# Output weights split by VectorE and spread over the attention's tail and the merge, with the first columns of two token tiles first

## The chip, the cores and the metric

The kernel runs on one NeuronCore of a Trainium2 chip. The metric is device microseconds of one execution; lower is better. Rows of the profile name the engines PE (TensorE matmul), PEld (TensorE weight load), DVE (VectorE), ACT (ScalarE), POOL (GpSimd) and SP (SyncE, which here only issues DMAs); a q behind a name (SPq, ACTq) is the engine's issuing queue.

## The reference, cut to what matters

```python
merged = sigmoid(g_conv) * y_conv + sigmoid(g_att) * y_att      # y_att = (att * silu(z_att)) @ w_att_out
x = x + gate * (merged @ w_o[layer])                            # 1024 tokens x 1024 columns, depth 1
return _rmsnorm(x, final_g)                                     # over each token's 1024 columns
```

Ahead of this stand a norm, one wide input projection, a convolution branch and an attention branch with 3 dilation groups of 8 heads. Everything is float32.

## The kernel before, in words

**Split operands.** A float32 product is made of three matmuls on fp32r tiles. Each operand is split into a high part (`hi`, a rounding copy on ACT, L57) and a low part (`lo = raw - hi`, a subtraction, L58, on DVE or, where `lo_eng` says so, on POOL); PE then adds hi*hi, hi*lo and lo*hi into one PSUM tile. Every weight block takes this road: SP loads it into a `wraw` buffer (three of them, used in turn), ACT writes `whi`, DVE or POOL writes `wlo`, and only then is the `wraw` buffer free for the next load.

**The last three stages.**

1. *The attention's tail.* PE's order is written by hand in slots; the other engines' order is made by a scheduler. After the last scores PE runs the gate projections (L73 to L75, tiles `whi`, `wlo`), with POOL making `wlo`. Beside them DVE combines the last head pair's three groups, in two halves of 512 tokens: `rd` is loaded (L885), reduced to `pr` (L897 to L922), four PE transposes of `pr` (L926) follow at a fixed place in PE's order, and from them come the last parts of `ah` and `al` (the attended rows' high and low parts).
2. *The merge* (`for d in range(KT)`). Per block `d` of 128 output features: 24 matmuls (two halves of 512 tokens, 12 each) of `w_ao[d]` with `ah`, `al`; per half DVE multiplies with the gate (L1034, `sgr`), adds the convolution's part (L1035, `ttr`), ACT writes `hh` and DVE `hl` (the merged rows' parts). DVE also makes the next block's `wlo`. `sgr` and `ttr` are loaded two blocks ahead, into four buffers of the tag `tmp`.
3. *The output* (`for t in range(8)`). For each tile `t` of 128 tokens, two halves `n` of 512 columns, each of 24 matmuls (L1059 to L1061): `hh`, `hl` of all 8 blocks k against the parts `oh`, `ol` of `w_o[n, kp]` with kp = k // 2. Then DVE and ACT apply gate, residual and norm (L1062 to L1074), and SP stores.

**The output weights before.** `w_out(n, kp)` loads one block of 128 x 1024, splits it with the low part on POOL, and is called for n = 0 at d = 1, 3, 5, 7 of the merge (tiles of their own) and for n = 1, four times, behind the merge (in the tiles of `ah` and `al`, tags s0 to s3, which the merge reads up to its end).

Of the kernel before, what the change touches and what calls it, by code (L numbers as in the profile page):

```python
# [8 lines left out]
F32 = mybir.dt.float32  # L9
F32R = mybir.dt.float32r  # L10
I32 = mybir.dt.int32
AF = mybir.ActivationFunctionType
# [4 lines left out]
P = 128  # L17
S = 1024
D = 1024
KT = 8  # L20
# [19 lines left out]
def layer(ctx: ExitStack, tc: tile.TileContext, a, out):  # L40
    nc = tc.nc
# [10 lines left out]
    def sbuf_pool(name, **kw):  # L52
        return tc.tile_pool(name=name, bufs=1, reuse_waits="tile", **kw)

    def split(hi, lo, raw, lo_eng=None):

        nc.scalar.activation(hi, raw, AF.Copy)  # L57
        (lo_eng or nc.vector).tensor_sub(lo, raw, hi.bitcast(F32))  # L58

    def load_raw(src, n=1024):  # L60
        raw = wpool.tile([P, n], F32, name="wraw", tag="wraw", bufs=3)
        nc.sync.dma_start(raw, src)
        return raw
# [16 lines left out]
    hh = const.tile([P, KT, S], F32R, name="hh")  # L80
    hl = const.tile([P, KT, S], F32R, name="hl")
# [37 lines left out]
    def bank():  # L119
        return pd.tile([P, 512], F32, name="d", tag="d")  # L120
# [50 lines left out]
    with sbuf_pool("start") as st, tc.manual_schedule(  # L171
# [125 lines left out]
        for raw in u_raw[0:2]:  # L297
            hi = wpool.tile([P, 1024], F32R, name="whi", tag="whi")
            lo = wpool.tile([P, 1024], F32R, name="wlo", tag="wlo")
# [35 lines left out]
        hi = st.tile([P, 1024], F32R, name="u2h", tag="tot")  # L335
        lo = st.tile([P, 1024], F32R, name="u2l", tag="vs", bufs=1)
# [3 lines left out]
        for kt in range(KT):  # L340
# [9 lines left out]
            c = slice(kt * P, (kt + 1) * P)  # L350
            for i, (wh, wl) in enumerate(u_w):
                for half in range(2):
                    s = slice(half * 512, half * 512 + 512)
# [121 lines left out]
    class Glu:  # L475
# [19 lines left out]
        def units(self):  # L495
            return [Unit(KT + self.ct, self.sig), Unit(self.ct, self.glu, HALF)]
# [127 lines left out]
    for d in range(KT):  # L624
        w, sg_ = ahead
# [19 lines left out]
    stk = ctx.enter_context(sbuf_pool("stacked"))  # L645
    ap_ = c_ctx.enter_context(sbuf_pool("att"))

    def pair_tile(n, name, dt=F32R):
        return stk.tile([P, 2, S], dt, name=name, tag=f"s{n}")
# [108 lines left out]
    def pieces():  # L758

        source = units()  # L760
        ahead = next(source)
        while ahead:
            (hi, lo), consume = ahead
            ahead = next(source, None)
            for half in range(2):
                s = slice(half * 512, half * 512 + 512)
                ps = bank()
                for k in range(KT):
                    c = slice(k * P, (k + 1) * P)
                    mm3(ps, hi[:, c], lo[:, c], hh[:, k, s], hl[:, k, s], k == 0, k == KT - 1)  # L770
                    if k == 3:
                        yield
                yield lambda half=half, s=s, ps=ps: consume(half, s, ps)
# [162 lines left out]
    def att_parts(j, s, raw):  # L936

        if j // 2 not in ah:
            ah[j // 2], al[j // 2] = pair_tile(j // 2, "ah"), pair_tile(2 + j // 2, "al")
        split(ah[j // 2][:, j % 2, s], al[j // 2][:, j % 2, s], raw)  # L940

    stream = pieces()


# [6 lines left out]
    with tc.manual_schedule(engines={nc.tensor.engine}):  # L951
        for slot_ in range(-LEAD, (2 * len(order) + KT) * 4 - LEAD):
            due, made[:] = made[:], []
            after = next(stream)
            for x in due:
                move_kq(*x)
                if x == (0, 1):
                    load_low(0)
            if 0 <= slot_ < stages:
                n, st_ = divmod(slot_, 8)  # L960
                if st_ == 0:
                    heads[n] = Attend(n)
                if st_ == 4 and n + 1 < len(order):
                    load_low(n + 1)
                heads[n].scores(st_)
            if TURN <= slot_ < stages + TURN:
                n, st_ = divmod(slot_ - TURN, 8)
                heads[n].turn(st_)
            if VAL <= slot_ < stages + VAL:
                n, st_ = divmod(slot_ - VAL, 8)  # L970
                heads[n].values(st_)
                if st_ == 7:
                    del heads[n]
                    j, g = order[n]
                    if g == 2:
                        for half, steps in enumerate((FIRST, SECOND)):
                            c = combine(j, half)
                            for x in steps:
                                beside.setdefault(slot_ + x, []).append(c)
            for c in beside.pop(slot_, ()):  # L980
                next(c)
            for c in late:
                for x in (2, 2, 3):
                    beside.setdefault(slot_ + x, []).append(c)
            late[:] = []
            j = slot_ - stages - VAL
            if 0 <= j < 3:
                raw = load_raw(atscr[j])
                for half in range(2):
                    s = slice(half * 512, half * 512 + 512)  # L990
                    att_parts(j, s, raw[:, s])
            if j == 11:
                ahead = weights(a["w_ao"][0], 512)
            if after:
                after()
        assert not beside and next(stream, None) is None
# [2 lines left out]

    pd = ctx.enter_context(psum_pool("pd3", bufs=8))  # L1000
    fp = ctx.enter_context(sbuf_pool("fin"))
    woh, wol, w1 = {}, {}, [None, None]

    def w_out(n, kp):
        raw = load_raw(a["w_o"][n, kp])
        if n:
            if kp % 2 == 0:
                w1[0:2] = pair_tile(kp // 2, "oh1"), pair_tile(2 + kp // 2, "ol1")
            hi, lo = (t[:, kp % 2] for t in w1)
        else:  # L1010
            hi, lo = (fp.tile([P, 1024], F32R, name=f"{x}{kp}") for x in ("oh", "ol"))
        split(hi, lo, raw, nc.gpsimd)
        woh[n, kp], wol[n, kp] = hi, lo

    def temp4(name):
        return fp.tile([P, S], F32, name=name, tag="tmp", bufs=4)

# [7 lines left out]
    for d in range(KT):  # L1025
        w, (sg_, tt) = ahead
        if d + 1 < KT:
            ahead = weights(a["w_ao"][d + 1], 512), gates_load(d + 1)
        if d % 2:
            w_out(0, d // 2)  # L1030
        hi, lo = hh[:, d, :], hl[:, d, :]

        def merge(half, s, ps):
            nc.vector.tensor_mul(sg_[:, s], ps, sg_[:, s])  # L1034
            nc.vector.tensor_add(tt[:, s], tt[:, s], sg_[:, s])  # L1035
            split(hi[:, s], lo[:, s], tt[:, s])

        project(w, merge, 4, lambda k, s: ah[k // 2][:, k % 2, s], lambda k, s: al[k // 2][:, k % 2, s])


    for kp in range(4):
        w_out(1, kp)
    gate_b = fp.tile([P, D], F32, name="gate_b")
    nc.sync.dma_start(gate_b, gscr.to_broadcast([P, D]))
    fg_b = fp.tile([P, D], F32, name="fg_b")
    nc.sync.dma_start(fg_b, a["final_g"].to_broadcast([P, D]))
    for t in range(8):
        xt, y = temp4("xt"), temp4("y")
        nc.sync.dma_start(xt, a["x"][t * P:(t + 1) * P, :])
        ss = fp.tile([P, 3], F32, name="ss", tag="ss", bufs=2)  # L1050
        cuts = (0, 512, 1024) if t < 7 else (0, 512, 768, 1024)
        for n, (c0, c1) in enumerate(zip(cuts, cuts[1:])):
            s = slice(c0, c1)
            ps = bank()[:, 0:c1 - c0]
            for k in range(KT):
                c = slice(t * P, (t + 1) * P)
                o = (k % 2) * 512 + c0 % 512
                rh, rl = (w[c0 // 512, k // 2][:, o:o + c1 - c0] for w in (woh, wol))
                nc.tensor.matmul(ps, hh[:, k, c], rh, start=k == 0, stop=False)  # L1059
                nc.tensor.matmul(ps, hh[:, k, c], rl, start=False, stop=False)  # L1060
                nc.tensor.matmul(ps, hl[:, k, c], rh, start=False, stop=k == KT - 1)  # L1061
            nc.vector.tensor_mul(y[:, s], ps, gate_b[:, s])  # L1062
            nc.vector.tensor_add(y[:, s], y[:, s], xt[:, s])
            nc.scalar.activation(xt[:, s], y[:, s], AF.Square, accum_out=ss[:, n:n + 1])
        r = fp.tile([P, 1], F32, name="r", tag="r", bufs=2)
        tmp = fp.tile([P, 3], F32, name="tmp3", tag="tmp3", bufs=2)
        nc.vector.tensor_add(r, ss[:, 0:1], ss[:, 1:2])
        if t == 7:
            nc.vector.tensor_add(r, r, ss[:, 2:3])
        nc.vector.tensor_scalar(r, r, 1.0 / D, EPS, op0=mult, op1=add)  # L1070
        inv_sqrt(r, 1, tmp)
        for n in range(2):
            s = slice(n * 512, n * 512 + 512)
            nc.vector.scalar_tensor_tensor(y[:, s], y[:, s], r, fg_b[:, s], op0=mult, op1=mult)  # L1074
            nc.sync.dma_start(out[t * P:(t + 1) * P, s], y[:, s])


# [64 lines left out]
```

## Time and profile before

| what | value |
|---|---|
| median of 3 timed runs | 1287.0 us (1286.51 to 1288.05) |
| the profiled execution's own time | 1284.9 us |
| its span, first to last instruction | 1283.1 us |
| PE busy in the span | 1251.0 us (97%) |
| DVE, ACT, POOL busy | 895.0, 476.3, 114.6 us |
| granted TensorE clock, mean | 0.999 of full speed |

Matmuls are pipelined: one of 512 columns is shown with 0.39 us, but the next starts 0.23 us behind it where nothing is missing. So the time that PE loses is read from the distance of starts. "Idle before" is the time in which an engine waited, with what ended it.

### The profile page before, as it was taken

The numbers are of one execution on the slowest core, as the hardware profiler recorded it, in microseconds if no ns is written. First come the engines' busy times: TensorE is split into PE (matmuls) and PEld (weight loads), VectorE is DVE, ScalarE is ACT, GpSimd is POOL, SyncE is SP. The second block draws the span as 40 slices with busy tenths as digits, with TensorE's granted clock in tenths as the row PEclk, the third lists the DMA queues.
The fourth block names the chain that finished last, engine by engine and source line by source line (L and its number), as shares of the span: only waits on it lengthen the run. The fifth ranks groups of instructions, "written<-read, shape, count | busy, mean of one in ns | idle before, by whom it ended". The sixth has DMA issues, their size and how long they took to land.

```text
span 1283.1 us, 16610 instructions
## 1 busy us (share of the span) xinstructions
PE 1251.0 (97%) x6148; PEld 1050.6 (82%) x6148; DVE 895.0 (70%) x1568; ACT 476.3 (37%) x911; POOL 114.6 (9%) x86
## 2 busy tenths in 40 slices
PE   6999999999999999999999999999999989999997
PEld 4777888888888888888788888888888878887786
DVE  6777999999999986853245545766666654348544
ACT  4653112111222146620115545445545458333211
POOL 0000000000000000000132111111111002202200
PEclk9999999999999999999999999999999999999999
DMA  9522311211211122555675565576675565558322
GB/s 367 180 97 73 109 66 57 91 52 47 94 55 50 50 74 74 165 183 188 143 182 125 125 159 142 156 179 150 153 207 126 147 181 177 151 203 286 117 96 69
DMA packets 85525, 171.53 MB, mean 134 GB/s; under 512 B 11202, under 2 KB 41026, under 8 KB 85444
## 3 DMA queue, kind: packets, MB, share of 16 engines
q1 hardware_dynamic: 69024, 157.66, 42.1%
q10 hardware_dynamic: 16420, 12.80, 3.2%
q8 instruction: 49, 0.80, 0.3%
q14 instruction: 32, 0.26, 0.1%
HBM read 105.74 MB, written 33.23 MB: 108 GB/s over the span
## 4 chain that ended last, share of the span: by engine, by line
PE 86%; DVE 5%; DMA 3%; issue 2%; ACT 2%; SPq 1%; POOL 1%; POOLq 0%; ACTq 0%; DVEq 0%
PE d L73 20%; PE d L74 20%; PE d L75 20%; PE o L875 4%; PE d L466 2%; PE d L467 2%; PE d L465 2%; PE d L1060 2%; PE d L1061 2%; PE t L860 2%; PE d L1059 2%; PE s L844 1%; PE s L843 1%; PE d L249 1%; PE d L247 1%
## 5 line engine op out<-in xcount | busy, mean ns | idle before, releaser
L73 PE MATMUL d<-hh,whi 128*128 128x512 f32 x1072 | 428.0, 399 | 1.8 <-DVE rot L710 0.9
L74 PE MATMUL d<-hl,whi 128*128 128x512 f32 x1072 | 418.0, 390 | 1.8 <-DVE hl L347 1.8
L75 PE MATMUL d<-hh,wlo 128*128 128x512 f32 x1072 | 419.1, 391 | 0.0
L406 DVE SCALAR_TENSOR_TENSOR v<-u,cw,v 128x1024 f32<-128x1024 f32 x232 | 280.7, 1287 | 0.0
L75 PEld LDWEIGHTS d<-hh,wlo 128*128 128x128 f32 x1072 | 201.3, 188 | 43.7 <-POOL wlo L58 0.7
L74 PEld LDWEIGHTS d<-hl,whi 128*128 128x128 f32 x1072 | 201.9, 188 | 41.6 <-DVE hl L347 2.6
L73 PEld LDWEIGHTS d<-hh,whi 128*128 128x128 f32 x1072 | 201.8, 188 | 41.3 <-DVE rot L710 1.5
L57 ACT ACTIVATE whi<-wraw 128x512 fp32r<-128x512 f32 (+1 forms) x107 | 87.9, 834 | 272.6 <-PE d L74 236.0
L58 POOL TENSOR_TENSOR wlo<-wraw,whi 128x512 fp32r<-128x512 f32 (+1 forms) x56 | 84.5, 1525 | 659.1 <-ACT whi L57 557.2
L852 ACT ACTIVATE sb<-sb,nm 128x128 f32<-128x128 f32 (+1 forms) x192 | 85.0, 444 | 86.3 <-DVE nm L850 82.0
L847 DVE CUSTOM_DVE_ANT_0 sb<-s,mask 128x128 f32<-128x128 f32 (+1 forms) x192 | 59.8, 347 | 61.1 <-PE s L844 54.9
L875 PE MATMUL o<-vt,pt 128*128 128x64 f32 x560 | 73.5, 267 | 1.6 <-ACT pt L863 1.0
L875 PEld LDWEIGHTS o<-vt,pt 128*128 128x128 f32 x560 | 70.2, 192 | 2.6 <-ACT pt L863 1.3
L58 DVE TENSOR_TENSOR wlo<-wraw,whi 128x1024 fp32r<-128x1024 f32 (+1 forms) x51 | 60.2, 1183 | 15.1 <-ACT whi L57 14.6
L1060 PE MATMUL d<-ol,hh 128*128 128x512 f32 (+1 forms) x136 | 51.6, 380 | 3.0 <-POOL ol L58 3.0
L844 PE MATMUL s<-k,ql 128*128 128x128 f32 (+1 forms) x192 | 51.0, 279 | 2.9 <-DMA ql<-kqp 2.9
L1059 PE MATMUL d<-oh,hh 128*128 128x512 f32 (+1 forms) x136 | 51.4, 378 | 0.1
L1061 PE MATMUL d<-oh,hl 128*128 128x512 f32 (+1 forms) x136 | 51.4, 378 | 0.0
L467 PE MATMUL d<-vh,hl 128*128 128x512 f32 x128 | 49.8, 389 | 0.0
L73 PE MATMUL d<-uh,whi 128*128 128x512 f32 x128 | 49.8, 389 | 0.0
L466 PE MATMUL d<-vl,hh 128*128 128x512 f32 x128 | 49.8, 389 | 0.0
L74 PE MATMUL d<-ul,whi 128*128 128x512 f32 x128 | 49.8, 389 | 0.0
(213 smaller groups left out, 1738.6 us busy)
## 6 DMA issues: line engine op xcount, KB each, us to landing
wraw<-in_w_t SPq DMA_DIRECT2D x67, 512.0 KB, 4.1
k<-kqp SPq DMA_DIRECT2D x96, 128.0 KB, 2.6
q<-kqp SPq DMA_DIRECT2D x96, 128.0 KB, 2.4
wa<-in_w_ada SPq DMA_DIRECT2D x16, 512.0 KB, 5.9
rd<-oscr SPq DMA_DIRECT2D x8, 792.0 KB, 5.6
ql<-kqp SPq DMA_DIRECT2D x48, 128.0 KB, 2.4
wraw<-in_w_v SPq DMA_DIRECT2D x11, 512.0 KB, 3.6
x<-in_xT SPq DMA_DIRECT2D x8, 512.0 KB, 10.2
```

The lines of the kernel that those rows point to most:

```text
L57: nc.scalar.activation(hi, raw, AF.Copy)
L58: (lo_eng or nc.vector).tensor_sub(lo, raw, hi.bitcast(F32))
L73: nc.tensor.matmul(ps, lh, rh, start=start, stop=False)
L74: nc.tensor.matmul(ps, lh, rl, start=False, stop=False)
L75: nc.tensor.matmul(ps, ll, rh, start=False, stop=stop)
L406: nc.vector.scalar_tensor_tensor(d, u[:, k:k + S], cw[:, ct, k:k + 1], d, op0=mult, op1=add)
L466: nc.tensor.matmul(ps, hh[:, k, ts_], rl, start=False, stop=False)
L852: nc.scalar.activation(sb[:, c:c + w], sb[:, c:c + w], AF.Exp, bias=nm[:, t - tp:t - tp + 1], scale=SCALE, accum_out=ov[:, t, h, 64:65])
L875: nc.tensor.matmul(self.po[:, t % 4, h], pt[:, c + i:c + i + P], self.vt[:, kb, r], start=i == 0, stop=i + P == w)
L1059: nc.tensor.matmul(ps, hh[:, k, c], rh, start=k == 0, stop=False)
L1060: nc.tensor.matmul(ps, hh[:, k, c], rl, start=False, stop=False)
L1061: nc.tensor.matmul(ps, hl[:, k, c], rh, start=False, stop=k == KT - 1)
```

## The change

`w_out` keeps its three steps (load, high part on ACT, low part), but the low part goes to DVE in all eight blocks. Three blocks, (n, kp) = (0,0), (0,1), (0,2), are made in the attention's tail, at the hand-written slots j = 4, 6 and 8, in tiles that the attention no longer reads (those of `ql`, tags s4 and s5, and the two `vt` buffers). At d = 1, 3, 5 of the merge follow (0,3), (1,0), (1,1); behind the merge's code (1,2) and (1,3), the last in the tile of `ah[0]` (tag s0). The output's first four pieces are ordered (t, n) = (0,0), (1,0), (0,1), (1,1) in place of (0,0), (0,1), (1,0), (1,1); `ss` gets three buffers.

```diff
--- before.py
+++ after.py
@@ -939,6 +939,25 @@
             ah[j // 2], al[j // 2] = pair_tile(j // 2, "ah"), pair_tile(2 + j // 2, "al")
         split(ah[j // 2][:, j % 2, s], al[j // 2][:, j % 2, s], raw)
 
+    woh, wol, pairs = {}, {}, {}
+
+    def w_out(n, kp, pool=None):
+
+        raw = load_raw(a["w_o"][n, kp])
+        if pool:
+            hi, lo = (pool.tile([P, 1024], F32R, name=f"{x}{n}{kp}") for x in ("oh", "ol"))
+        elif kp < 2:
+            if not pairs:
+                pairs.update({i: pair_tile(4 + i, "oh") for i in range(2)})
+            hi, lo = pairs[0][:, kp], pairs[1][:, kp]
+        elif n:
+            both = pair_tile(0, "o13")
+            hi, lo = both[:, 0], both[:, 1]
+        else:
+            hi, lo = (stk.tile([P, 1024], F32R, name=x, tag="vt", bufs=2) for x in ("oh", "ol"))
+        split(hi, lo, raw)
+        woh[n, kp], wol[n, kp] = hi, lo
+
     stream = pieces()
 
 
@@ -989,6 +1008,8 @@
                 for half in range(2):
                     s = slice(half * 512, half * 512 + 512)
                     att_parts(j, s, raw[:, s])
+            if j in (4, 6, 8):
+                w_out(0, j // 2 - 2)
             if j == 11:
                 ahead = weights(a["w_ao"][0], 512)
             if after:
@@ -999,19 +1020,6 @@
 
     pd = ctx.enter_context(psum_pool("pd3", bufs=8))
     fp = ctx.enter_context(sbuf_pool("fin"))
-    woh, wol, w1 = {}, {}, [None, None]
-
-    def w_out(n, kp):
-        raw = load_raw(a["w_o"][n, kp])
-        if n:
-            if kp % 2 == 0:
-                w1[0:2] = pair_tile(kp // 2, "oh1"), pair_tile(2 + kp // 2, "ol1")
-            hi, lo = (t[:, kp % 2] for t in w1)
-        else:
-            hi, lo = (fp.tile([P, 1024], F32R, name=f"{x}{kp}") for x in ("oh", "ol"))
-        split(hi, lo, raw, nc.gpsimd)
-        woh[n, kp], wol[n, kp] = hi, lo
-
     def temp4(name):
         return fp.tile([P, S], F32, name=name, tag="tmp", bufs=4)
 
@@ -1026,8 +1034,8 @@
         w, (sg_, tt) = ahead
         if d + 1 < KT:
             ahead = weights(a["w_ao"][d + 1], 512), gates_load(d + 1)
-        if d % 2:
-            w_out(0, d // 2)
+        if d in (1, 3, 5):
+            w_out(*((0, 3), (1, 0), (1, 1))[d // 2], fp)
         hi, lo = hh[:, d, :], hl[:, d, :]
 
         def merge(half, s, ps):
@@ -1038,30 +1046,35 @@
         project(w, merge, 4, lambda k, s: ah[k // 2][:, k % 2, s], lambda k, s: al[k // 2][:, k % 2, s])
 
 
-    for kp in range(4):
-        w_out(1, kp)
+    w_out(1, 2, fp)
+    w_out(1, 3)
     gate_b = fp.tile([P, D], F32, name="gate_b")
     nc.sync.dma_start(gate_b, gscr.to_broadcast([P, D]))
     fg_b = fp.tile([P, D], F32, name="fg_b")
     nc.sync.dma_start(fg_b, a["final_g"].to_broadcast([P, D]))
-    for t in range(8):
-        xt, y = temp4("xt"), temp4("y")
-        nc.sync.dma_start(xt, a["x"][t * P:(t + 1) * P, :])
-        ss = fp.tile([P, 3], F32, name="ss", tag="ss", bufs=2)
-        cuts = (0, 512, 1024) if t < 7 else (0, 512, 768, 1024)
-        for n, (c0, c1) in enumerate(zip(cuts, cuts[1:])):
-            s = slice(c0, c1)
-            ps = bank()[:, 0:c1 - c0]
-            for k in range(KT):
-                c = slice(t * P, (t + 1) * P)
-                o = (k % 2) * 512 + c0 % 512
-                rh, rl = (w[c0 // 512, k // 2][:, o:o + c1 - c0] for w in (woh, wol))
-                nc.tensor.matmul(ps, hh[:, k, c], rh, start=k == 0, stop=False)
-                nc.tensor.matmul(ps, hh[:, k, c], rl, start=False, stop=False)
-                nc.tensor.matmul(ps, hl[:, k, c], rh, start=False, stop=k == KT - 1)
-            nc.vector.tensor_mul(y[:, s], ps, gate_b[:, s])
-            nc.vector.tensor_add(y[:, s], y[:, s], xt[:, s])
-            nc.scalar.activation(xt[:, s], y[:, s], AF.Square, accum_out=ss[:, n:n + 1])
+    rows, ys, sums_ = {}, {}, {}
+
+    def out_cols(t, n, c0, c1):
+
+        if t not in ys:
+            rows[t], ys[t] = temp4("xt"), temp4("y")
+            nc.sync.dma_start(rows[t], a["x"][t * P:(t + 1) * P, :])
+            sums_[t] = fp.tile([P, 3], F32, name="ss", tag="ss", bufs=3)
+        xt, y, s = rows[t], ys[t], slice(c0, c1)
+        ps = bank()[:, 0:c1 - c0]
+        for k in range(KT):
+            c = slice(t * P, (t + 1) * P)
+            o = (k % 2) * 512 + c0 % 512
+            rh, rl = (w[c0 // 512, k // 2][:, o:o + c1 - c0] for w in (woh, wol))
+            nc.tensor.matmul(ps, hh[:, k, c], rh, start=k == 0, stop=False)
+            nc.tensor.matmul(ps, hh[:, k, c], rl, start=False, stop=False)
+            nc.tensor.matmul(ps, hl[:, k, c], rh, start=False, stop=k == KT - 1)
+        nc.vector.tensor_mul(y[:, s], ps, gate_b[:, s])
+        nc.vector.tensor_add(y[:, s], y[:, s], xt[:, s])
+        nc.scalar.activation(xt[:, s], y[:, s], AF.Square, accum_out=sums_[t][:, n:n + 1])
+
+    def out_norm(t):
+        y, ss = ys.pop(t), sums_[t]
         r = fp.tile([P, 1], F32, name="r", tag="r", bufs=2)
         tmp = fp.tile([P, 3], F32, name="tmp3", tag="tmp3", bufs=2)
         nc.vector.tensor_add(r, ss[:, 0:1], ss[:, 1:2])
@@ -1073,6 +1086,17 @@
             s = slice(n * 512, n * 512 + 512)
             nc.vector.scalar_tensor_tensor(y[:, s], y[:, s], r, fg_b[:, s], op0=mult, op1=mult)
             nc.sync.dma_start(out[t * P:(t + 1) * P, s], y[:, s])
+
+
+    for t, n in ((0, 0), (1, 0), (0, 1), (1, 1)):
+        out_cols(t, n, n * 512, n * 512 + 512)
+        if n:
+            out_norm(t)
+    for t in range(2, 8):
+        cuts = (0, 512, 1024) if t < 7 else (0, 512, 768, 1024)
+        for n, (c0, c1) in enumerate(zip(cuts, cuts[1:])):
+            out_cols(t, n, c0, c1)
+        out_norm(t)
 
 
 # ---- launch: one core; the host only lays the arrays out ----
```

The change also moves instructions that it does not name, since the scheduler orders DVE, ACT and SP. Three places follow; names are those of the tiles.

SP in the attention's tail, before: `in_w_t` are gate weights, `in_w_ao` the merge's weights, `rd` the last head pair's rows.

```order
L62 DMA wraw<-atscr_95 128x1024
L62 DMA wraw<-in_w_t 128x1024 x2
L62 DMA wraw<-in_w_ao 128x512
L885 DMA rd<-oscr_4282 128x4x396
L62 DMA wraw<-in_w_ao 128x512
L885 DMA rd<-oscr_4282 128x4x396
```

The same place now:

```order
L62 DMA wraw<-atscr_95 128x1024
L62 DMA wraw<-in_w_t 128x1024
L62 DMA wraw<-in_w_o 128x1024 x2
L885 DMA rd<-oscr_4282 128x4x396
L62 DMA wraw<-in_w_t 128x1024
L62 DMA wraw<-in_w_o 128x1024
L62 DMA wraw<-in_w_ao 128x512 x2
L885 DMA rd<-oscr_4282 128x4x396
```

Two blocks of `w_o` stand ahead of the first `rd`, and the third block and one more `in_w_ao` ahead of the second.

DVE at the combination of the last head pair, first half, now (before, the rows are the same without those of L58, whose first names are the output weights' parts in the tiles of `ql` and `vt`):

```order
L58 TENSOR_TENSOR oh<-wraw,oh 128x1024 x2
L897 TENSOR_TENSOR ma<-rd 128x8
L898 TENSOR_TENSOR ma<-ma,rd 128x8
L902 TENSOR_TENSOR w<-rd,ma 128x8 x3
L908 TENSOR_TENSOR wd<-w,rd 128x8 x3
L909 TENSOR_TENSOR wd<-wd 128x8
L910 TENSOR_TENSOR wd<-wd 128x8
L911 RECIPROCAL wd<-wd 128x8
L913 TENSOR_TENSOR w<-w,wd 128x8 x3
L917 TENSOR_TENSOR rd<-rd,w 128x4x2x64 x3
L58 TENSOR_TENSOR ol<-wraw,oh 128x1024
L920 TENSOR_TENSOR rd<-rd 128x4x2x64
```

Two low parts moved in ahead of the chain that makes `pr`, and a third into it; `pr` (L922) is the row behind the last one.

DVE at blocks d = 4 and 5 of the merge in the new kernel, with tile numbers (`wlo_9433` is the merge's weight block 6, `ol11` and `ol12` are low parts of (1,1) and (1,2), `ttr_9343` and `sgr_9342` belong to d = 4, 9392 and 9393 to d = 5):

```order
L58 TENSOR_TENSOR ol11_9443<-wraw_9440,oh11_9442 128x1024
L58 TENSOR_TENSOR hl_65<-ttr_9343,hh_64 128x512
L1042 TENSOR_TENSOR sgr_9342<-d_9413,sgr_9342 128x512
L58 TENSOR_TENSOR wlo_9433<-wraw_9430,whi_9432 128x512
L1043 TENSOR_TENSOR ttr_9343<-ttr_9343,sgr_9342 128x512
L1042 TENSOR_TENSOR sgr_9392<-d_9446,sgr_9392 128x512
L58 TENSOR_TENSOR hl_65<-ttr_9343,hh_64 128x512
L1043 TENSOR_TENSOR ttr_9393<-ttr_9393,sgr_9392 128x512
L1042 TENSOR_TENSOR sgr_9392<-d_9463,sgr_9392 128x512
L58 TENSOR_TENSOR hl_65<-ttr_9393,hh_64 128x512
L1043 TENSOR_TENSOR ttr_9393<-ttr_9393,sgr_9392 128x512
L58 TENSOR_TENSOR wlo_9483<-wraw_9480,whi_9482 128x512
```

The low part of (1,1), which was POOL's, now stands ahead of the weights of block 6 in DVE's queue, so that `wlo_9433` waits for whatever `ol11` waits for; `ol12` is the row behind `wlo_9483`, the weights of block 7. In the same way the low part of (1,3) stands ahead of the first `hl` of d = 7, three rows before the merge's last `ttr`.

## Rows read from the trace of the kernel before

**Rows 1.** Windows: length; busy PE, PEld, DVE, ACT, POOL; clock; DMA share; GB/s.

```profile
1138.00:1183.40 45.40, 44.02 (x193) 35.78 (x192) 36.14 (x48) 16.81 (x26) 9.66 (x4) 1.00 0.83 284
1183.40:1198.40 15.00, 11.97 (x48) 8.29 (x47) 10.24 (x9) 6.09 (x9) 10.53 (x4) 1.00 0.57 191
```

**Rows 2.** Timeline of PE: start, length, line, operation, tiles, idle before.

```profile
1137.88 0.39 PE L73 MATMUL d<-ah,whi 128*128 128x512 f32 x1
...
1170.74 0.39 PE L74 MATMUL d<-al,whi 128*128 128x512 f32 x1
...
1183.42 0.39 PE L1059 MATMUL d<-oh,hh 128*128 128x512 f32 x1
...
1198.35 0.40 PE L1060 MATMUL d<-ol,hh 128*128 128x512 f32 x1
```

**Rows 3.** Waits of PE's weight loads, 1138 to 1284 us: total, times, longest.

```profile
PEld d L1060 <- POOL ol L58: 4.3, 3, 1.6
PEld d L75 <- DVE wlo L58: 2.2, 2, 1.8
PEld d L1059 <- ACT hh L57: 0.5, 1, 0.5
PEld d L1061 <- DVE hl L58: 0.4, 1, 0.4
```

**Rows 4.** Timeline of POOL.

```profile
1166.98 2.40 POOL L58 TENSOR_TENSOR ol<-wraw,oh 128x1024 fp32r<-128x1024 f32 x1 [8.44 <-ACT oh L57]
...
1189.37 8.13 POOL L58 TENSOR_TENSOR ol<-wraw,oh 128x1024 fp32r<-128x1024 f32 x3 [2.24 <-ACT oh L57]
```

**Rows 5.** Timeline of DVE in the merge.

```profile
1167.45 2.47 DVE L58 TENSOR_TENSOR hl<-ttr,hh 128x512 fp32r<-128x512 f32 x1 [0.65 <-ACT hh L57]
1169.85 0.68 DVE L1035 TENSOR_TENSOR ttr<-ttr,sgr 128x512 f32<-128x512 f32 x1
1170.45 0.68 DVE L58 TENSOR_TENSOR wlo<-wraw,whi 128x512 fp32r<-128x512 f32 x1
...
1174.52 2.48 DVE L58 TENSOR_TENSOR hl<-ttr,hh 128x512 fp32r<-128x512 f32 x1 [0.68 <-ACT hh L57]
...
1185.06 2.61 DVE L1035 TENSOR_TENSOR ttr<-ttr,sgr 128x512 f32<-128x512 f32 x1
```

**Rows 6.** Line 58 over the whole span: duration in ns, min/median/max.

```profile
L58 DVE TENSOR_TENSOR wlo<-wraw,whi x51: 676/1222/2883, 51.6 to 1177.5; 128x1024 fp32r<-128x1024 f32 x43, 128x512 fp32r<-128x512 f32 x8
```

**Rows 7.** The high part of an output block on ACT: count, busy, mean ns.

```profile
L57 ACT ACTIVATE oh<-wraw 128x1024 fp32r<-128x1024 f32 x8 | 8.3, 1053 | 6.9 <-DMA wraw<-in_w_o 4.4 <-DMA ascr<-gs 2.4
```

**Rows 8.** DMA issues from 1138 to 1200 us: count, KB, us to landing.

```profile
wraw<-in_w_o SPq DMA_DIRECT2D x7, 512.0 KB, 5.4
```

**Rows 9.** Timeline of SP: DMA issues.

```profile
1096.49 0.33 SPq L62 DMA_DIRECT2D wraw<-in_w_ao  x1
1099.80 0.38 SPq L885 DMA_DIRECT2D rd<-oscr  x1
...
1160.61 0.38 SPq L62 DMA_DIRECT2D wraw<-in_w_o  x1
```

**Rows 10.** Timeline of DVE in the attention's tail.

```profile
1104.99 0.17 DVE L897 TENSOR_TENSOR ma<-rd 128x8 f32<-128x8 f32 x1 [15.18 <-DMA rd<-oscr]
...
1112.05 0.69 DVE L922 TENSOR_TENSOR pr<-rd 128x512 f32<-128x512 f32 x1
```

**Rows 11.** Timeline of PE in the attention's tail.

```profile
1117.88 0.60 PE L926 MATMUL t<-ident,pr 128*128 128x128 f32 x4
```

**Rows 12.** Timeline of ACT in the attention's tail.

```profile
1108.45 1.28 ACT L729 ACT_TABLE_LOAD   x1 [0.25 <-ACT w L903]
1109.91 0.60 ACT L729 ACTIVATE gs<-d 128x512 f32<-128x512 f32 x1 [0.17 <-PE d L75]
...
1115.18 1.06 ACT L57 ACTIVATE whi<-wraw 128x1024 fp32r<-128x1024 f32 x1 [4.67 <-PE d L74]
```

**Rows 13.** The chain that ended last: start, length.

```profile
1275.33 0.13 PE d L1061
```

## Prediction

> **What bounds the kernel now.** I began with the busy time of each engine, in two stretches: the merge (1138 to 1183.4) and the output's start (1183.4 to 1198.4). In the merge PE is busy for 44.02 of 45.40 us and DVE for 36.14; at the output's start PE for 11.97 of 15.00, with POOL at 10.53 [rows 1]. PE is the bound, so the change is worth what PE loses where it acts, and no more. The time that PE loses is read from its timeline. From 1137.88 to 1170.74 it makes 145 steps, 0.2266 us each [rows 2], which is its pace with nothing missing. The merge has 192 matmuls: 43.5 us at that pace, and the output starts after 45.5 (1183.42). So the merge loses 2.0. From 1183.42 to 1198.35 there are 46 steps: 10.4 us at that pace, 14.9 in fact [rows 2]. So the output's start loses 4.5. Together 6.5 us, the most that this change can give back: behind that PE runs to its last matmul at 1275.33 [rows 13], and that stretch and the last tile's norm have the same work as before.
>
> The waits of the weight loads name the causes: 4.3 us for `ol` from POOL, 2.2 for `wlo` from DVE, 0.5 and 0.4 for `hh` and `hl` [rows 3]. (They add up to 7.4, since a weight load runs ahead of its matmul; the 6.5 of the steps is what counts.) Then I looked at the two engines named.
>
> POOL: a low part takes 2.40, and the last three run in one piece of 8.13 us from 1189.37 to 1197.50 [rows 4]. These are blocks (1,1) to (1,3), which PE wants from half a tile after the output's start. DVE: where POOL works, a subtraction of 512 columns takes 2.47, 2.48 or 2.61 us in place of 0.68 [rows 5]. The one at 1167.45 began while POOL ran (1166.98 to 1169.38) and ended at 1169.92, about its own length behind POOL's end. So DVE stands still while POOL subtracts, and loses about 1.8 us each time. Behind the two long `hl` stand `ttr` and `wlo`, and for that `wlo` PE waits in the merge; behind the long `ttr` at 1185.06 stand the last `hh` and `hl`.
>
> The Trainium skill, page "SBUF — State Buffer", section Who interferes with whom, says that VectorE's operations with two SBUF inputs and GpSimd's reads share a port under an exclusive lock, and that the loser blocks fully; by that rule the 1.8 us go away with POOL's eight operations, and the trace agrees (2.47 against 0.68).
>
> **What each part does, step by step.**
>
> *The low parts on DVE.* One of 1024 columns takes 1.22 us on DVE (median of 51 rows, 43 of them that wide), at the worst 2.88 beside POOL [rows 6]. Eight are 9.8 us more for DVE: three in the attention's tail, five from the merge on. Against that, up to the weights of block 7 DVE loses three standstills (2.88 - 0.68 [rows 6], 2.47 - 0.68 and 2.48 - 0.68 [rows 5]: 5.8 us), and takes on only (0,3), which is made while DVE has nothing to do yet, (1,0) and (1,1): 2.4 us in its way. So `wlo` should come some 3 us earlier than before. It was late by 2.0 in all. I take this wait as gone: 2.0 us.
>
> *The last `hh`, `hl`.* In the old order the `ttr` of 2.61 us stood ahead of them [rows 5]. Now the low part of (1,3) does. Its tile is that of `ah[0]`, which PE last reads with the sixth matmul of the merge's last half: 1137.88 + 43.5 - 2.7 + 1.4 = 1180.1. ACT's 1.05 [rows 7] and DVE's 1.22 bring it to about 1182.4, `hl` to 1183.1. PE, without the merge's loss, starts the output at 1181.4 and wants that `hl` with the 24th matmul, 1186.6. It has 3.5 us to spare; the loss here goes too.
>
> *The new order of the output's pieces.* (0,0) and (1,0) need blocks (0,0) to (0,3) alone, all split before the output starts. Blocks n = 1 are wanted 48 steps behind the start, 1192.3, not 24; the last of them, (1,3), at 36 steps plus that, 1196 to 1197 (its k are the seventh and eighth of eight), 14 us behind its 1182.4. So all of POOL's waits go, about 4.5 with the `hh`, `hl`. The order by itself would hide some 5.4 us of lateness (24 steps); it is the reserve of this term.
>
> *The three blocks in the attention's tail.* Nothing in the trace of before has an output block there, so this cost is bounded. Below: nothing, since the tail's slack covers it. Above: DVE's chain to `pr` starts when `rd` lands (1104.99) and ends at 1112.74 [rows 10]; PE wants `pr` at 1117.88 [rows 11], 5.1 us later. In that chain stands one new low part, 1.22. Ahead of it stand two, whose second load takes the place of one issued at 1096.49 [rows 9]; a load of that size lands after 5.4 us (median under the merge's load [rows 8]): 1101.9, ACT to 1102.9, DVE to 1104.2, before `rd` lands. `rd` itself, issued at 1099.80 [rows 9], may land a little later behind the larger load; with 1 us for that, 2.9 us are left. With twice the landing time (10.8) the low part ends at 1109.5, `pr` 9.0 us later (7.75 + 1.22) at 1118.5, and PE waits 0.6. I take 0, nearest to the rows, and keep 0.6 as the upper end. The third block's high part waits on ACT ahead of a gate's `gs` (1109.91 [rows 12]), which frees one of two PSUM banks. Its load can be issued when the second low part is done, 1104.2, so it lands at 1109.6, and `gs` ends near 1112.5 (1.05, a table load of 1.28 and 0.60 behind). PE wants that bank when the half that it then runs ends, 1115.1 (ACT waits for that same end at 1115.18 [rows 12]): hidden, with 2.6 us left.
>
> **Sum.** 2.0 + 4.5 + 0 = 6.5 us. The profiled execution took 1284.9 us, 1.8 more than its span of 1283.1; it would take 1278.4. The three timed runs lie higher, median 1287.0, so in their terms the new time is 1280.5, 0.5% less. A change of 0.2% (2.6 us) is about what a measurement of this kernel can tell from none; the three runs spread over 1.5 us.
>
> **The rivals.**
>
> *A. As summed.* All three waits go. 1280.5; I give it 0.60, own range 1279 to 1282.
>
> *B. DVE's queue takes over a part of the merge's wait.* The low part of (1,1) now stands ahead of block 6's `wlo`, and waits for a load that comes through a queue in its third place in the merge. Its counterpart was issued at 1160.61 [rows 9]. 5.4 us to landing, 1.05 on ACT, 1.22, then `hl` and `sgr` at 0.60 each (the distance of starts at 1169.85 and 1170.45 [rows 5]) and `wlo` at 0.68 give 1170.2; PE wants it with the third matmul of block 6, 1137.88 + 32.6 + 0.5 = 1171.0. Only 0.8 us are left, so a landing 2 us later costs 1.2 there, and the next block can repeat it. For it: the DMA engines are 83% busy in the merge [rows 1]. Against it: one `w_o` load fewer competes there by then, and SP's buffers come free earlier, with no POOL step of 2.40 before them. Price up to the old 2.0: 1282.5. Chance 0.20.
>
> *C. DVE is too full.* 36.14 of 45.40 us are busy already [rows 1]. If four low parts (4.9 us) came on top with nothing going off, DVE would have 41.0 for 43.5, its lag would last through the merge, and the `hh`, `hl` loss (about 0.6) and the merge's 2.0 would stay, with as much again for a last `wlo`: gain 2 us, 1285. Against it, the 5.8 us of standstill do go off. The Trainium skill, page "Trace Analysis", section Optimizing Scalar/DVE Operations, would move work the other way, to ScalarE or even GpSimd, when VectorE is saturated (it adds that the shared port may spoil that); by that rule this change could not help the merge, and the trace speaks against the rule here by its rows of 2.47. Chance 0.12, half of it within 0.2%.
>
> *D. Slower: the transposes of `pr` wait.* If the attention's tail loads land so late that `pr` misses 1117.88, PE, in its hand-written order, stands still with all gate work behind it. The bound above gives 0.6 us for a doubled landing; it decides only from there plus 6.5, that is, a load that takes some 17 us. Three times the usual landing is far from any row; I give 0.04 for this and another 0.04 for what I do not see; at, say, 8 us of waiting, 1288.5.
>
> **How the numbers follow.** The prediction is A's, 1280.5. Down: no row allows more than 6.5, so only the runs' spread is left, 1278.5. Up: B (1282.5) and the nearer half of C, to 1285.0; beyond lie D, half of C and some spread, under 0.2. Faster by over 0.2%: A, B and half of C, 0.85; same: the other half of C and a little of D's, 0.08; slower: 0.07.
>
> **What would show it.** Right: POOL idle once the last gate weights are split; no DVE row of `hl`, `ttr` or `wlo` over 0.7 us in the merge; PE's first output matmul near 1181.4 and the next 100 at 0.2266 us; PE waits for neither `ol` nor `wlo`; transposes near 1117.9. Wrong: a wait for `wlo` at block 6 or 7 with `ol` ahead of it on DVE (B), `hl` of d = 7 late (C), or idle time before L926 (D).

## The result, and the profile after

The changed kernel takes 1278.35 us (median of 6 runs, 1277.03 to 1279.77), the kernel before in the same session 1286.39 (6 runs, 1283.56 to 1288.05). The ratio is 0.994, interval 0.9927 to 0.9954: 5.9 to 9.4 us less. The forecast was 6.5 less. The profiled executions say where: the span went from 1283.1 to 1275.9, 7.2 us.

Windows of the kernel after, of the same two stages (length; busy PE, PEld, DVE, ACT, POOL; clock; DMA share; GB/s):

```profile
1138.00:1181.40 43.40, 43.40 (x193) 35.96 (x192) 37.00 (x56) 17.90 (x27) 0.00 (x0) 1.00 0.90 311
1181.40:1197.00 15.60, 15.60 (x70) 12.92 (x69) 6.03 (x9) 2.28 (x6) 0.00 (x0) 1.00 0.14 45
```

PE is busy throughout in both, and POOL does nothing; compare [rows 1]. DVE has 56 instructions in the merge where it had 48, for 0.9 us more of busy time. Line 58's durations on DVE (ns: min/median/max), with 2883 as the longest in [rows 6], say why:

```profile
L58 DVE TENSOR_TENSOR wlo<-wraw,whi x51: 680/1219/1227, 51.5 to 1172.4; 128x1024 fp32r<-128x1024 f32 x43, 128x512 fp32r<-128x512 f32 x8
```

The timeline of PE (start, length, line, operation, tiles):

```profile
1137.23 0.39 PE L73 MATMUL d<-ah,whi 128*128 128x512 f32 x1
...
1170.10 0.39 PE L74 MATMUL d<-al,whi 128*128 128x512 f32 x1
...
1180.75 0.39 PE L1069 MATMUL d<-oh,hh 128*128 128x512 f32 x1
...
1191.17 0.39 PE L1070 MATMUL d<-ol,hh 128*128 128x512 f32 x1
```

These answer to [rows 2]. The merge's 192 matmuls take 43.5 us (45.5 before), the 46 steps behind the output's start 10.4 (14.9 before). So 2.0 and 4.5 came back, and the waits of [rows 3] are gone: from 1094 to 1284 us the view of waits has no row for PE or its weight loads. The remaining 0.65 of the 7.2 lies ahead of the change: the merge begins at 1137.23, not 1137.88. PE is 0.17 ahead at 1061 already and has the rest by 1063.9, behind a wait for the attention's `pt` of 0.54 in place of 1.04, and the first load of an output block goes out at 1089.18. So I count it as scatter between executions, not as gain. In the five experiments below that have the same early blocks and no work added on DVE before the merge it begins between 1137.7 and 1138.2, and once at 1140.62 (the second run with idle POOL work); the last section shows one source of that spread.

POOL's last row of the kernel after, and DVE's rows at the places of [rows 5]:

```profile
1115.66 2.39 POOL L58 TENSOR_TENSOR wlo<-wraw,whi 128x1024 fp32r<-128x1024 f32 x1 [8.47 <-ACT whi L57]
```

```profile
1164.91 1.23 DVE L58 TENSOR_TENSOR ol<-wraw,oh 128x1024 fp32r<-128x1024 f32 x1 [1.11 <-ACT oh L57]
1166.06 0.69 DVE L58 TENSOR_TENSOR hl<-ttr,hh 128x512 fp32r<-128x512 f32 x1
1166.66 0.68 DVE L1042 TENSOR_TENSOR sgr<-d,sgr 128x512 f32<-128x512 f32 x1
1167.26 0.68 DVE L58 TENSOR_TENSOR wlo<-wraw,whi 128x512 fp32r<-128x512 f32 x1
...
1180.85 1.22 DVE L58 TENSOR_TENSOR o<-wraw,o 128x1024 fp32r<-128x1024 f32 x1
1181.99 0.69 DVE L58 TENSOR_TENSOR hl<-ttr,hh 128x512 fp32r<-128x512 f32 x1
```

An output block's low part costs DVE 1.22, and the `hl` behind it 0.69 where it was 2.47. Block 6's `wlo` is done at 1167.94, 2.4 us before PE wants it (1137.23 + 32.6 + 0.5 = 1170.3).

The tail, which the forecast took as free: timelines of DVE and of PE.

```profile
1106.03 1.20 DVE L897 TENSOR_TENSOR ma<-rd 128x8 f32<-128x8 f32 x1 [1.65 <-DMA rd<-oscr]
...
1111.06 1.21 DVE L58 TENSOR_TENSOR ol<-wraw,oh 128x1024 fp32r<-128x1024 f32 x1
...
1112.91 0.69 DVE L922 TENSOR_TENSOR pr<-rd 128x512 f32<-128x512 f32 x1
```

```profile
1117.23 0.60 PE L926 MATMUL t<-ident,pr 128*128 128x128 f32 x4
```

`pr` is done at 1113.60, 3.6 us before its transposes ([rows 10, 11]: 5.1). The new low part stands ahead of it, and `ma` took 1.20 in place of 0.17: POOL was splitting gate weights from 1104.79 to 1107.19.

### The profile page after: what moved, and what is told of

Its sections match the earlier page's. It is cut to its first block, busy times and chain, and to the rows that moved or that the text cites. A ratio compares the mean times of both kernels' runs of the same rounds, so it can differ in the third digit from the quotient of the medians.

```text
span 1275.9 us, 16604 instructions
## 1 busy us (share of the span) xinstructions
PE 1248.6 (98%) x6148; PEld 1050.6 (82%) x6148; DVE 890.5 (70%) x1576; ACT 476.8 (37%) x911; POOL 94.7 (7%) x78
## 4 chain that ended last, share of the span: by engine, by line
PE 91%; DVE 4%; DMA 2%; ACT 2%; issue 1%; SPq 0%; ACTq 0%; DVEq 0%
PE d L73 22%; PE d L75 22%; PE d L74 22%; PE o L875 4%; PE d L1070 2%; PE d L1069 2%; PE d L467 2%; PE d L466 2%; PE d L1071 2%; PE d L465 2%; PE t L860 2%; PE s L844 1%; PE s L843 1%; PE d L249 1%; PE d L247 1%; PE d L248 1%
## 5 line engine op out<-in xcount | busy, mean ns | idle before, releaser
L58 POOL TENSOR_TENSOR wlo<-wraw,whi 128x512 fp32r<-128x512 f32 (+1 forms) x56 | 84.8, 1529 | 658.0 <-ACT whi L57 556.2
L58 DVE TENSOR_TENSOR wlo<-wraw,whi 128x1024 fp32r<-128x1024 f32 (+1 forms) x51 | 57.9, 1137 | 15.6 <-ACT whi L57 15.0
L465 PE MATMUL d<-vh,hh 128*128 128x512 f32 x128 | 49.8, 389 | 0.0
L75 PE MATMUL d<-uh,wlo 128*128 128x512 f32 x128 | 49.8, 389 | 0.0
L632 DVE TENSOR_TENSOR gs<-d,sgc 128x512 f32<-128x512 f32 x16 | 11.1, 691 | 54.9 <-PE d L75 48.8
```

Source lines behind the costliest of these rows:

```text
L75: nc.tensor.matmul(ps, ll, rh, start=False, stop=stop)
L465: nc.tensor.matmul(ps, hh[:, k, ts_], rh, start=k == 0, stop=False)
```

## The experiments

P is the theory of the prediction: POOL's subtractions hold DVE up and come late. O says that the new order and the early blocks alone carry the gain. Each time has the interval of its ratio to the kernel before, which was run with it (1286.0 to 1286.3).

**Low parts back on POOL**, all else as changed.

```diff
-        split(hi, lo, raw)
+        split(hi, lo, raw, nc.gpsimd)
```

> The changed kernel (same early blocks, same new order of the output) with the eight low parts of the output weights back on POOL. Theory P (POOL's subtractions hold DVE up, and that made the merge's loss): the standstills of DVE return, three or four of about 1.8 us in the merge, against 2.4 us of low parts that leave DVE before the weights of block 7; DVE's wlo comes some 3 us later than in the changed kernel, where it had about 2.4 to spare, so PE waits 0.5 to 2 us for wlo: 1279 to 1281. Rival O (order and early placement alone carry the gain, the engine does not matter): no DVE row over 0.7 us is needed for it, PE waits for nothing, 1278.4.

1282.88 us (ratio 0.9961 to 0.9983): 4.5 us of the gain are gone, more than P said. POOL and DVE of this run:

```profile
1168.88 2.39 POOL L58 TENSOR_TENSOR ol<-wraw,oh 128x1024 fp32r<-128x1024 f32 x1 [7.89 <-ACT oh L57]
```

```profile
1169.35 2.47 DVE L58 TENSOR_TENSOR hl<-ttr,hh 128x512 fp32r<-128x512 f32 x1 [0.70 <-ACT hh L57]
1171.74 0.68 DVE L1043 TENSOR_TENSOR ttr<-ttr,sgr 128x512 f32<-128x512 f32 x1
1172.35 0.68 DVE L58 TENSOR_TENSOR wlo<-wraw,whi 128x512 fp32r<-128x512 f32 x1
```

And its waits of PE from 1094 us on (total, times, longest):

```profile
PE d L75 <- DVE wlo L58: 3.6, 2, 1.8
```

This is how a standstill reaches PE: POOL starts, the `hl` beside it takes 2.47, the `wlo` behind it ends at 1173.03, and PE, which wanted it at 1171.13, goes on at 1173.08. The same happens one block later. By the steps PE loses 4.4 in the merge and 0.7 at the output's start. No wait is for `ol`: the lateness of POOL's own results is gone, its hold on DVE is not.

**The new order alone**, in the kernel before (the loop over `(0, 0), (1, 0), (0, 1), (1, 1)`, nothing else).

> The old kernel with only the output's first four pieces reordered to (0,0), (1,0), (0,1), (1,1). Theory P: the waits for ol (3.8 us between 1189 and 1198) go, since blocks n = 1 are wanted 5.4 us later than before and the three were late by about 1 each; the merge's 2.0 and the 0.6 for hh, hl stay: 3.8 us less than before, 1282.6. Rival O: the whole gain, 6.5 us, 1279.9 or less.

1281.86 us (0.9952 to 0.9975). The waits of PE from 1094 us on:

```profile
PE d L75 <- DVE wlo L58: 2.6, 2, 1.6
```

The order hides POOL's late results wholly (3.8 us of `ol` waits by the steps), but the merge's loss stays and is 3.2 by the steps, 2.0 before.

**The low parts on DVE alone**, in the kernel before (`split` without `nc.gpsimd`).

> The old kernel, old places and old order of the output, with only the eight low parts moved from POOL to DVE. Theory P: the merge's 2.0 and the 0.6 for hh, hl go, since no DVE operation stands still; the n = 1 blocks come at DVE's 1.22 us instead of POOL's 2.40 in a row, and the last one, whose load waits for the first one's buffer, ends near 1189.7, about 1 us before PE wants it at 1190.9 in the old order; so 5.5 to 6.5 us less than before, 1280 to 1281. Rival O: the n = 1 blocks stay late, since placement and order are the old ones: at most 2 us less than before, 1284.4 or more.

1278.86 us (0.9933 to 0.9957), within the scatter of the whole change. PE waits for nothing from 1094 us on. O falls: it allowed a gain of 2 us. The expectation of P was too high by 1 to 2: it allowed for a gain of 5.5 to 6.5, and the medians give 7.3. The profiled executions of this run and of the kernel before begin the merge within 0.04 us of each other, and their spans differ by 6.5 (1276.6 and 1283.1), which is the sum read from the steps.

**The whole change with the old order.**

```diff
-    for t, n in ((0, 0), (1, 0), (0, 1), (1, 1)):
+    for t, n in ((0, 0), (0, 1), (1, 0), (1, 1)):
```

> The changed kernel with the output's first four pieces in the old order (0,0), (0,1), (1,0), (1,1). Theory P: blocks n = 1 are then wanted from 1186.2, (1,3) near 1190.2; its low part ended at 1182.07 in the changed kernel, so nothing waits and the time is that of the changed kernel, 1278.4 within 0.5. Rival O: the ol waits return, about 3.8 us more, 1282.

1278.55 us (0.9928 to 0.9952): as P said. The order is a reserve that nothing draws on once DVE makes the low parts.

**All blocks out of the tail**: the three early ones at d = 0, 2 and 4 of the merge.

```diff
-            if j in (4, 6, 8):
-                w_out(0, j // 2 - 2)
...
+        if d in (0, 2, 4):
+            w_out(0, d // 2)
```

> The kernel after, with the three output blocks of the attention's tail taken back into the merge (d = 0, 2, 4): six blocks are split in the merge. Theory M (DVE has room once POOL is silent): three low parts of 1.22 us come on top of 37.0 us of DVE work in 43.4, and block 6's wlo had 2.4 us to spare, so PE waits at most about 1 us: 1278.4 to 1279.5. Rival C of the prediction (DVE, or the queue of loads ahead of it, too full): the DMA engines were 90% busy there already and three more loads come on top, wlo is late for one or two blocks and the last hl too: 1281 or more.

1280.13 us (0.9945 to 0.9970), between the two. DVE before the one wait of PE, which is 0.7 for `wlo`:

```profile
1173.26 1.23 DVE L58 TENSOR_TENSOR ol<-wraw,oh 128x1024 fp32r<-128x1024 f32 x1 [1.00 <-ACT oh L57]
1174.40 0.68 DVE L58 TENSOR_TENSOR hl<-ttr,hh 128x512 fp32r<-128x512 f32 x1
1175.00 0.69 DVE L1043 TENSOR_TENSOR ttr<-ttr,sgr 128x512 f32<-128x512 f32 x1
1175.61 0.68 DVE L58 TENSOR_TENSOR wlo<-wraw,whi 128x512 fp32r<-128x512 f32 x1
```

This is rival B's mechanism, one weight block later: DVE stands idle for 1.00 in front of the low part of (1,1), whose load is late, and the `wlo` behind it is that of block 7. PE loses 1.3 by the steps, 1.0 of it here. So the early placement is worth 1.3 us by the steps (1.8 by the medians, whose intervals overlap) when the merge would else carry six blocks; with four in the merge and four behind it (the run with DVE alone) it is worth nothing.

**POOL busy with work that nobody uses.** The kernel after, DVE making the low parts, and beside four of them a subtraction on POOL whose result a later load overwrites. In the second run the added line is `tensor_sub(fg_b, raw, hi.bitcast(F32))`, in the third `tensor_copy(fg_b, raw)`.

```diff
         split(hi, lo, raw)
+        if pool:
+            nc.gpsimd.tensor_sub(fg_b, hi.bitcast(F32), hi.bitcast(F32))
```

First: 

> The kernel after, with a subtraction on POOL added for each of the four blocks (0,3), (1,0), (1,1), (1,2): same size as a low part, its inputs are the high part alone, its result is not used (a load overwrites it) and it holds no raw buffer. Standstill: DVE rows of 2.4 us and more come back at these four places. If the standstill alone made the loss of the run with POOL's low parts (4.5 us): 1281 to 1283. If the loss came from the standstill and the raw buffers that POOL holds together: the standstill of 1.8 us eats most of the 2.4 us that wlo has to spare, PE waits 0 to 0.5 us: 1278.4 to 1279. If neither POOL nor buffers but the lateness of POOL's own results was the cause: 1278.4, and no long rows on DVE.

Second: 

> As the run with POOL's unused subtractions, but they read the raw block and the high part, as a low part does, so the raw buffer is free only when POOL is done. Standstill alone: the same time as that run. Standstill with the ring of three raw buffers: loads in the merge are issued 2 to 4 us later than in the kernel after, wlo is late at blocks 6 and 7, about 1281 to 1283 as with POOL's low parts. Lateness of results only: 1278.4.

Third: 

> As the run in which POOL's unused subtractions read the raw block and the high part, but POOL copies the raw block instead (one input in place of two, the same four places, the result unused). If any pass of POOL over SBUF holds DVE: DVE rows of over 2 us at the four places, PE waits for wlo as there, 1281 to 1284. If only a subtraction of POOL does: DVE's rows stay at 0.68 and 1.22 us, the raw buffers alone are held longer, 1278.4 to 1279.5.

1280.53 us (0.9947 to 0.9974), 1283.28 (0.9972 to 0.9991) and 1278.14 (0.9926 to 0.9951). POOL and DVE of the first:

```profile
1159.26 2.07 POOL L960 TENSOR_TENSOR fg_b<-oh 128x1024 f32<-128x1024 f32 x1 [13.55 <-ACT oh L57]
1169.07 2.87 POOL L960 TENSOR_TENSOR fg_b<-oh 128x1024 f32<-128x1024 f32 x1 [7.74 <-ACT oh L57]
```

```profile
1159.50 2.92 DVE L58 TENSOR_TENSOR ol<-wraw,oh 128x1024 fp32r<-128x1024 f32 x1
...
1168.96 1.23 DVE L58 TENSOR_TENSOR ol<-wraw,oh 128x1024 fp32r<-128x1024 f32 x1 [0.21 <-ACT oh L57]
1170.10 2.38 DVE L58 TENSOR_TENSOR hl<-ttr,hh 128x512 fp32r<-128x512 f32 x1
...
1173.00 0.68 DVE L58 TENSOR_TENSOR wlo<-wraw,whi 128x512 fp32r<-128x512 f32 x1
```

No result of POOL is awaited here, and the long DVE rows are back, and with them a wait of 2.31 for `wlo`. All five executions of the first run (1280.16 to 1282.80) are slower than all six of the kernel after (1277.03 to 1279.77). So POOL's passes cost time without any lateness. Neither size fits: the time lies between "standstill alone" and "0 to 0.5".

The profiles show the way rather than the usual size, since they are of the slowest execution of the first run and of the second (1287.38, where the median is 1283.28). In the first, block 6's `wlo` comes 4.8 us later behind the merge's first matmul than in the kernel after, 2.4 more than it has to spare. Of these 4.8, 2.4 were there before the two long rows: a gate load took 6.9 us to land where the kernel after shows 4.6 (`ttr`, issued at 1149.32 and 1148.08), and whether POOL had a hand in that stays open. The two long rows add 1.7 each, and about 1 is taken up, since in the kernel after DVE stood idle for 1.11 ahead of the second of these low parts. By this sum PE's wait needed the holds and the late load together in this execution.

Two things were not reckoned with. A held DVE frees a gate's tile later, so SP issues the loads behind it later. The `hl` behind the first long row ends at 1163.02, and then SP goes on:

```profile
1163.04 0.32 SPq L1032 DMA_DIRECT2D ttr<-cscr  x1
1163.41 0.42 SPq L62 DMA_DIRECT2D wraw<-in_w_o  x1
```

The second row is the load of (1,1), whose low part stands ahead of block 6's `wlo`: 25.2 us behind the merge's first matmul, where the kernel after has 21.2 (1158.38) and the second run 25.7. And PE's clock fell after the wait (below). How much of the second run's further 2.7 us is the raw buffer, how much POOL's longer rows there (2.57 to 3.44) and how much the clock was not separated.

The third run's copy takes POOL 1.04, and DVE beside it is held for up to 0.9:

```profile
1164.72 1.04 POOL L960 COPY fg_b<-wraw 128x1024 f32<-128x1024 f32 x1 [8.48 <-DMA wraw<-in_w_o]
```

```profile
1164.77 1.54 DVE L1046 TENSOR_TENSOR ttr<-ttr,sgr 128x512 f32<-128x512 f32 x1
```

So a one-input pass holds DVE too; both theories of that run missed, since the first took its length for that of a subtraction. Held for so little, `wlo` still has time to spare, and PE waits for nothing. This run has the same tiles as the first two, so the tile that POOL writes is not what costs them time.

**The tail's slack.** First the third early block's low part done seven times, then, since most of those repeats were placed behind `pr`, the addition that makes `pr` eleven times.

```diff
+        if (n, kp) == (0, 2):
+            for _ in range(6):
+                nc.vector.tensor_sub(lo, raw, hi.bitcast(F32))
```
```diff
+        for _ in range(11 if (j, half) == (3, 0) else 1):
             nc.vector.tensor_add(pr, o[0], o[1])
```

> The kernel after, with the low part of the third early block written seven times instead of once (six more subtractions of 1.14 us from start to start, ahead of pr on DVE, 6.8 us). Theory T: pr was ready 3.6 us before its transposes, so PE waits 3.2 us in front of line L926 and all of it reaches the end: 1281.5. Rival: the delay is taken up elsewhere (pr's chain holds idle time, or gate work covers it): under 1279.5.

> The kernel after, with the addition that makes pr of the first half of the last head pair done eleven times (ten more at 0.6 us from start to start, 6.0 us, all of them ahead of the transposes). Theory T: pr had 3.6 us to spare, so it is ready at about 1119.6 in place of 1113.6, PE waits 2.4 us in front of line L926 and the end moves by as much: 1280.8. Rival: the wait is taken up by other work, or a second wait for gs behind it adds as much again: under 1279.3, or 1282.5 and more.

The first: 1280.84 us (0.9948 to 0.9973). One row of its DVE, and its wait of PE:

```profile
1115.94 0.69 DVE L922 TENSOR_TENSOR pr<-rd 128x512 f32<-128x512 f32 x1
```

```profile
PE d L73 <- ACT gs L729: 1.7, 1, 1.7
```

This execution is 2.0 us behind the kernel after before the added work, so `pr` was only 1.0 us later by it, and its transposes did not wait. The other five repeats stood ahead of `at` and of the weights of the next half, and a gate's `gs` stood behind those on ACT: PE waited 1.7 us for `gs`. It costs time, but by another wait than expected. The second: 1286.37 us (0.9989 to 1.0007), the whole gain gone. Its waits, then DVE and POOL:

```profile
PE t L927 <- DVE pr L923: 5.7, 1, 5.7
```

```profile
1113.84 10.05 DVE L923 TENSOR_TENSOR pr<-rd 128x512 f32<-128x512 f32 x11
```

```profile
1116.61 2.38 POOL L58 TENSOR_TENSOR wlo<-wraw,whi 128x1024 fp32r<-128x1024 f32 x1 [8.47 <-ACT whi L57]
```

The eleven took 10.05, not 6.7: 0.72 from start to start, and one of them 2.79 while POOL split gate weights. That is 9.36 more than one; less the slack of 3.6 that makes 5.7, the wait that is seen. So the slack is as read, and the theory's size failed by the added work. The end moved by 8.0, 2.3 more than the wait; the last section shows where 1.6 of that went.

## Why the prediction was right

**DVE's standstill, and POOL the cause: right, and shown.** DVE alone gives the whole gain, and POOL alone, with nobody waiting for its result, takes some of it back. The standstill is not all of it: of the 6.5, 3.8 were waits for POOL's own late results, which the new order alone hides, and 2.6 (the merge's 2.0, and 0.6 for `hh`, `hl`) came from the hold.

**The merge's 2.0 and the output's 4.5: right in the profiled execution to 0.1 us.** The time itself is 2.15 us below the 1280.5 forecast and 0.15 under the low end given. 0.6 of that is the kernel before, 1286.39 beside the change where the forecast had 1287.0; 1.5 is the gain, 8.0 by the medians, not 6.5. The interval of the gain goes from 5.9 on, the profiled pair adds only the 0.65 ahead of the change, and where a typical pair has the rest I cannot show. The 2.0 is not a fixed price: in the two runs that kept POOL's low parts the merge lost 3.2 and 4.4. It depends on when POOL's passes fall against `hl` and `wlo`, and that changes between executions too: the run with the new order alone has the merge of the kernel before, and in it POOL's third pass starts 30.1 us behind the merge's first matmul, not 29.1. That may be a part of the medians' 8.0, which isn't shown.

**The last `hh`, `hl`: right.** Forecast 1182.4 for the low part of (1,3) and 1183.1 for `hl`; 1182.07 and 1182.68 in fact, in a merge that began 0.65 earlier.

**The order as reserve: right.** Alone it hides POOL's lateness; with DVE it changes nothing. Two slips did no harm. The last quarter of (0,1), which needs (1,3), is 18 steps into that piece, not 36; the 1196 to 1197 given is the time for 18. And the 2.88 named as the worst for 1024 columns is a `wlo` of 512 (1156.20 in the kernel before), as the sum of the standstills has it.

**The tail at nothing: right, slack mis-sized in the safe direction, which was luck.** 3.6 us left, 2.9 estimated. The second `w_o` load took 6.2 us to land, 5.4 estimated, and its low part was done at 1104.38, before `rd`, as forecast. `rd` came 1 us later (1106.00), as the sum allowed, but less than half of that counted, since POOL's gate weights held DVE up to 1107.2 anyway; before the change they did so too (the first `w` of the chain took 2.53 at 1105.41).

**Rival B: its slack was too small.** 0.8 us estimated, 2.4 measured, since the load was issued at 1158.38, not 1160.61. SP issues it right behind a gate load that waits for DVE's `hl`, and that `hl` ended at 1157.97; before, it stood behind a `wlo` held for 2.88 and ended at 1159.69. With three more blocks in the merge the mechanism comes true, at 1.3 us.

**Rival C: out.** DVE has 37.00 of 43.40 us to do and PE does not wait. The run with DVE alone is 7.3 us faster than the kernel before, which makes the low parts on GpSimd. The rule of the Trainium skill (page "Perfetto Trace Analysis", section Optimizing Scalar/DVE Operations) that was weighed against the trace would have let them stay there; it is the rule's own caution, on the shared port, that the trace bears out.

**Rival D: mechanism right, price too low.** A late `pr` does stop PE. The prediction put a microsecond of waiting at a microsecond of time (8 us, from 1280.5 to 1288.5); 5.7 us of waiting cost 8.0.

## What to carry to other kernels

An engine that is "free" isn't, if its passes hold a busier one: look for rows of the busy engine that are longer than their kind by the free engine's remaining time, and price the move by those rows, not by the two engines' busy shares. When DVE seems too full to take work, count first what it loses to standstills. And separate what a helper does late from what it holds up: an order that hides the first leaves the second.

## What the runs showed of the hardware

**Who starts first holds the other.** In the rows above DVE's low part starts at 1159.50, 0.24 behind POOL, and takes 2.92 while POOL takes 2.07; at 1168.96 it starts 0.11 ahead of POOL, and now takes 1.23 while POOL takes 2.87. So the hold works both ways (POOL's row grows by 0.8, though DVE still had 1.1 to run; the rows don't show why). The Trainium skill, page "SBUF — State Buffer", section Who interferes with whom, describes such an exclusive lock; these rows agree, and so does the copy's 1.54.

**Not every DVE row is held.** All the long rows above have both inputs in SBUF. The product with the gate reads one of its two from PSUM (`d`), and beside POOL it takes its usual time. POOL and DVE of the kernel before, two products in 1.29 us:

```profile
1142.60 2.40 POOL L58 TENSOR_TENSOR ol<-wraw,oh 128x1024 fp32r<-128x1024 f32 x1 [23.89 <-ACT oh L57]
```

```profile
1143.75 1.29 DVE L1034 TENSOR_TENSOR sgr<-d,sgr 128x512 f32<-128x512 f32 x2 [4.48 <-DMA sgr<-ascr]
```

**A wait of PE can cost more than its length.** After 2.31 us of waiting in the first run with idle POOL work, and after 5.71 in the run with the late `pr`, the clock was granted at half, 1.2 GHz, and steps took 0.43 us in place of 0.23. Windows of these two, then of the run with low parts on POOL, after a wait of 1.83:

```profile
1173.75:1177.00 3.25, 3.25 (x8) 2.57 (x9) 3.06 (x6) 1.32 (x3) 0.00 (x0) 0.50 0.79 282
1177.50:1182.00 4.50, 4.50 (x22) 3.72 (x21) 4.50 (x5) 1.43 (x2) 2.06 (x1) 1.00 0.90 289
```

```profile
1124.20:1128.20 4.00, 4.00 (x12) 3.33 (x12) 1.38 (x2) 0.63 (x1) 0.00 (x0) 0.50 0.62 203
```

```profile
1180.70:1186.00 5.30, 5.30 (x23) 4.38 (x24) 3.97 (x6) 1.16 (x2) 0.00 (x0) 1.00 0.78 268
```

By the steps the low clock took about 1.6 us in each of the first two. In the second run with idle POOL work a wait of 2.72 was followed by more of it, about 2.9 us by the steps:

```profile
1177.00:1183.00 6.00, 6.00 (x14) 4.75 (x15) 5.81 (x9) 3.25 (x5) 1.23 (x1) 0.50 0.75 235
```

Length alone does not decide. In the attention, at about 1052, every profiled execution here has the same wait of PE for `ql`, 2.85 to 2.94 us long. In three (the kernel before, the kernel after, all blocks out of the tail) the clock stayed at 1.00 behind it; in the nine others it fell to half, for some 3 to 7 us. The kernel after, and the first run on the tail's slack:

```profile
1052.60:1058.00 5.40, 5.40 (x38) 4.91 (x39) 1.14 (x6) 1.22 (x5) 0.00 (x0) 1.00 1.00 253
```

```profile
1052.60:1058.00 5.40, 5.40 (x22) 4.92 (x22) 1.18 (x6) 1.04 (x5) 0.00 (x0) 0.50 1.01 258
```

From the end of that wait to the transposes of `pr` PE takes 64.7 to 65.2 us in the three and 65.3 to 67.1 in the others (the run with the late `pr` left out). So whether such a wait costs only its length changes from one execution to the next, and a microsecond or two between two single executions needs no cause in the kernel. In the profiled execution of the kernel before no wait in the changed stages was followed by a fall, so this is no part of the 6.5 that was read there; whether it is part of the medians' 8.0 is not shown.
